# A diffusion layer on one core: what VectorE and ScalarE do ahead of what at its beginning, and where the step decays of its scan are computed

## The chip, the cores and the metric

The kernel runs on one core of a Trainium2 chip. It is one launch. The metric is the device time of that launch in microseconds (us), the median of three runs; smaller is better. A core has five engines that run side by side, each on its own queue of instructions in order: TensorE (PE, matrix products), VectorE (DVE), ScalarE (ACT), GpSimd (POOL) and SyncE (SP, which here issues the transfers). They wait for each other by semaphores.

## The reference

One layer of a diffusion model, for 512 latent tokens and 128 context tokens of width 1024. Both are normed and modulated by a conditioning vector, run through three mixers side by side (attention, a gated short convolution, a bidirectional state-space scan called SSD), each gated, summed and projected; a SwiGLU feed-forward part follows.

```python
def trunk_layer(x, mod, latent, ...):
    shift1, scale1, gate1, shift2, scale2, gate2 = jnp.split(mod, 6, axis=-1)   # mod = silu(c) @ ada_w + ada_b
    h = rms_norm(x, norm1_g) * (1.0 + scale1) + shift1
    mixed, k, v, s = token_mixers(h, latent, ...)
    x = x + gate1 * mixed
    ...
def token_mixers(h, latent, ...):
    proj = h @ w_in
    (q, k, v, conv_bg, conv_cg, conv_x, z, xbc, dt_raw, gate_logits) = jnp.split(proj, ...)
    ...
    dt = jax.nn.softplus(dt_raw + ssd_dt_bias)          # step sizes, 64 per token (2 directions x 32 heads)
    a = -jnp.exp(ssd_a_log)
    y_f, s_f = ssd_chunked(xs, dt[:, :, 0], a[0], bm, cm, s0[:, 0])
    ...
def ssd_chunked(x, dt, a, bm, cm, s0):
    acs = jnp.cumsum(dt * a, axis=2)                    # per chunk of 128 tokens
    decay = jnp.exp(where(causal, acs_i - acs_j))
    to_end = jnp.exp(acs[:, :, -1:] - acs)
    chunk_decay = jnp.exp(acs[:, :, -1])
    ...
```

## The kernel before

**Data.** The 640 tokens stay in SBUF, transposed: width in 8 blocks of 128 partitions (`KB`), tokens along the free axis. For precision each factor of a product is held as two parts, a high part cast to fp32r and a low part that is what the cast left out; a product is then three matmuls (high·high, high·low, low·high). `split` makes the parts: a cast on ScalarE (L166) and a subtraction on VectorE (L167). Every weight that comes in as a raw tile (`wr`, `ws`) is split so into `wh` and `wl` before TensorE can use it.

**Order.** Most of the program is placed by a tile scheduler. In the beginning, `manual_schedule` makes TensorE, VectorE and ScalarE take their instructions in the order in which the code is written. SP issues loads in program order, and waits where a buffer isn't free.

**Beginning** (pool `start`, L397 to L494). The x blocks, the conditioning columns and one 1 MB modulation matrix for each block (`modulation_load`, tile `aw`) are loaded. The squares of x are summed, `rstd` makes the norm's factor per token, and `rowcast` spreads it over the partitions as the row `rr` (TensorE L349, then VectorE's copy L351). A loop over the 8 blocks in the order `ORDER` then has, in pass n:
- `products(n)`: 16 small matmuls of the modulation matrix (L438) and ScalarE's copy of their result, `ms` (L440);
- in pass 0 `rowcast`'s row;
- `parts_of(n-1)`: the high part of the normed block before (ScalarE L458) and its low part (VectorE L459);
- `scaled(n)`: x times rr on VectorE (L455);
- the matmuls of the first gate (`EARLY`) on block n-2 (`streamed`, L311);
- `factors(n)`: four small matmuls on ms (L446), two small VectorE rows for shift and scale (`mod` L447, `A` L449), and the normed block `hf`: 512 columns on ScalarE (L451), 128 on VectorE (L452).

The first gate's weights, two raw tiles of 512 KB, are loaded behind the second modulation matrix and split in pass 1, after block 0's parts. Those of a second gate (`PLAIN[0]`) are split in pass 5, and seven of its eight blocks (`fill`) are done in the last two passes.

**Step decays.** `decays` is a generator: every `yield` hands back to the code that draws it with `next`. It projects the step sizes on TensorE (L513), transposes them, takes the softplus by a series on VectorE with an exponential on ScalarE, sums them along each chunk by products with triangles of ones, and leaves `cd`, `nlc`, `dte` in SBUF and the rows D_a and D_e in DRAM, for the SSD stage alone. Its four scratch tiles come from the shared slots (`slot`, 128 x 640). In before all of it is drawn inside the gated conv, between conv's units.

**Conv and attention.** The conv's units multiply and convolve on VectorE (`uv`, `g`, L162, L589) and sum some weights' parts on GpSimd (L229). Attention follows in the pool `att`: K projection, V projection in five token blocks (its parts `vh`, `vl`; the last block also copied as `vo` and stored), then the four Q projections of two heads each. `heads_norm_rope` copies a token block, takes its norm (`rms`, `rr` on GpSimd) and rotates it (`raw`, `rot`); `q_T` and `keys_T` transpose on TensorE (L745) and split. `rot`, `vo` and the squares `sq` share three buffers (tag `tmp`).

Of the kernel before, what the change touches and what calls it, by code (L numbers as in the profile page):

```python
# [15 lines left out]
P = 128  # L16
D = 1024
KB = D // P
# [67 lines left out]
def layer_kernel(  # L86
# [6 lines left out]
    nc = tc.nc  # L93
# [302 lines left out]
    with tc.tile_pool(name="start", bufs=10, reuse_waits="tile") as sp:  # L396
# [14 lines left out]
        modulation_load(ORDER[0])  # L411
        nc.sync.dma_start(par, cols)
        modulation_load(ORDER[1])
        raws = [qraw(w_gt[EARLY], a) for a in range(2)]
# [42 lines left out]
        def parts_of(k):  # L457
            act.copy(h[k].hi, hf[k])  # L458
            dve.tensor_tensor(h[k].lo, hf[k], f32(h[k].hi), op=sub)  # L459
# [6 lines left out]
        fill = None  # L466
        for n in range(KB + 2):
            if n + 3 < KB:
                modulation_load(ORDER[n + 3])
            if n < KB:  # L470
                products(ORDER[n])
            if n == 0:
                rr = rowcast(rs, TOKBLKS, sp)
            if 1 <= n <= KB:
                parts_of(ORDER[n - 1])
            if n == 1:
                we = Quarters([qsplit(raw) for raw in raws])
                raws = [qraw(w_gt[PLAIN[0]], a) for a in range(2)]
            if n == 5:
                wf, fill = Quarters([qsplit(raw) for raw in raws]), acc()  # L480
                raws = [qraw(w_gt[PLAIN[1]], a) for a in range(2)]
            if n < KB:
                scaled(ORDER[n])
            if n >= 2:
                for m in range(2):
                    streamed(early[m], we, m, n - 2)
            if n < KB:
                factors(ORDER[n])
            if n == KB - 1:
                streamed(fill, wf, 0, *range(4))  # L490
            if n == KB:
                streamed(fill, wf, 0, *range(4, 7))
        nc.sync.dma_start(wdt, w_dt)
        nc.sync.dma_start(rws, rows.unsqueeze(0).to_broadcast([P, rows.shape[0]]))  # L494
# [8 lines left out]
    dve.tensor_scalar(cw2[:, 96:], pv_["xcb"], 0.5, None, op0=mult)  # L503

    def decays():
# [16 lines left out]
        t4 = [slot() for _ in range(4)]  # L522
# [24 lines left out]
        yield  # L547
        pa = mx()
# [7 lines left out]
        dve.tensor_copy(tot, pt[:, :N])  # L556
        yield
# [39 lines left out]
    with tc.tile_pool(name="pj", bufs=2, reuse_waits="tile") as pj:  # L597
# [71 lines left out]
        for i in range(4):  # L669
            for j, _ in enumerate(conv_units(i)):  # L670
                next(dec, None)
            if i % 2:
                gate_unit(*todo.pop(0))
                next(dec, None)
        run(dec)
# [11 lines left out]
    with tc.tile_pool(name="att", bufs=2, reuse_waits="tile") as ap:  # L687
        cs = ap.tile([P, 8 * P], F32, name="cs", bufs=1)
        nc.sync.dma_start(cs, consts[:, C_COS:])
# [849 lines left out]
```

## Time and profile before

| what | value |
|---|---|
| runs | 1725.39, 1725.76, 1726.85 us; median 1725.76 |
| profiled execution | 1725.58 us, of which the span of its instructions is 1723.8 |
| TensorE busy | 1688.1 us (98% of the span), 11826 matmuls |
| VectorE busy | 1295.2 us (75%), 2330 instructions |
| ScalarE busy | 762.5 us (44%), 1437 instructions |
| GpSimd busy | 289.9 us (17%), 257 instructions |

Busy means that an instruction of the engine was running; a TensorE that is busy may still run at its lower clock, which the columns named PEclk or clk tell (1.00 is 2.4 GHz, 0.50 is 1.2 GHz). "x" is a count of instructions. A row of the timeline ends in brackets with the idle time of the engine ahead of it, and the instruction that ended that time.

### The profile page before, as it was taken

The numbers are of one execution on the slowest core, as the hardware profiler recorded it, in microseconds if no ns is written. First come the engines' busy times: TensorE is split into PE (matmuls) and PEld (weight loads), VectorE is DVE, ScalarE is ACT, GpSimd is POOL, SyncE is SP. The second block draws the span as 40 slices with busy tenths as digits, with TensorE's granted clock in tenths as the row PEclk, the third lists the DMA queues.
The fourth block names the chain that finished last, engine by engine and source line by source line (L and its number), as shares of the span: only waits on it lengthen the run. The fifth ranks groups of instructions, "written<-read, shape, count | busy, mean of one in ns | idle before, by whom it ended". The sixth has DMA issues, their size and how long they took to land.

```text
span 1723.8 us, 30050 instructions
## 1 busy us (share of the span) xinstructions
PE 1688.1 (98%) x11826; PEld 1643.1 (95%) x11826; DVE 1295.2 (75%) x2330; ACT 762.5 (44%) x1437; POOL 289.9 (17%) x257
## 2 busy tenths in 40 slices
PE   6999999999999999999999999999999999999998
PEld 4889999999999999999999999999999999999998
DVE  5779785786546778878886589994578676757898
ACT  4534434565454655555555332312355332424442
POOL 0234441110001111111001000000001231323432
PEclk9999999999999999999999999999999999999999
DMA  8322334211243534454444589763441222222222
GB/s 329 116 77 89 124 102 135 80 41 61 75 141 104 162 117 143 144 158 136 139 153 135 180 302 307 260 219 98 154 147 47 95 74 86 74 86 95 67 74 97
DMA packets 126974, 225.05 MB, mean 131 GB/s; under 512 B 9200, under 2 KB 69488, under 8 KB 125808
## 3 DMA queue, kind: packets, MB, share of 16 engines
q1 hardware_dynamic: 126832, 223.12, 39.6%
q8 instruction: 93, 1.52, 0.4%
q14 instruction: 49, 0.40, 0.1%
HBM read 199.43 MB, written 23.66 MB: 129 GB/s over the span
## 4 chain that ended last, share of the span: by engine, by line
PE 84%; DVE 10%; issue 3%; ACT 1%; DMA 1%; POOL 1%; SPq 0%; DVEq 0%; POOLq 0%; ACTq 0%
PE acc L311 41%; PE mx L250 21%; PE mx L311 7%; DVE wl L167 2%; PE acc L1277 2%; PE mx L1012 2%; PE mx L964 2%; PE mx L1018 1%; PE acc L778 1%; PE mx L298 1%; PE mx L299 1%; PE mx L297 1%; PE mx L990 1%; PE acc L794 1%; PE mx L941 1%
## 5 line engine op out<-in xcount | busy, mean ns | idle before, releaser
L311 PE MATMUL acc<-h,wh 128*128 128x320 f32 x2528 | 480.8, 312 | 0.2 <-ACT s L583 0.2
L311 PEld LDWEIGHTS acc<-h,wh 128*128 128x128 f32 x2528 | 394.8, 188 | 3.2 <-issue 2.7
L166 ACT CAST wh<-wr 128x1024 fp32r<-128x1024 f32 (+2 forms) x224 | 217.0, 971 | 322.6 <-PE acc L311 139.6
L167 DVE TENSOR_TENSOR wl<-wr,wh 128x1024 fp32r<-128x1024 f32 (+2 forms) x224 | 274.4, 1227 | 97.2 <-ACT wh L166 95.8
L311 PE MATMUL acc<-h,wl 128*128 128x320 f32 x1264 | 289.1, 310 | 0.0
L311 PEld LDWEIGHTS acc<-h,wl 128*128 128x128 f32 x1264 | 211.9, 188 | 0.0
L250 PE MATMUL mx<-h,wh 128*128 128x320 f32 x824 | 183.5, 310 | 0.0
L250 PE MATMUL mx<-s,wh 128*128 128x320 f32 x720 | 159.7, 309 | 1.5 <-DVE g L162 1.3
L311 PE MATMUL acc<-s,wh 128*128 128x320 f32 x768 | 152.7, 309 | 0.0
L986 ACT ACTIVATE ex<-rw,nlc 128x128 f32<-128x128 f32 x320 | 102.7, 394 | 106.2 <-DVE M L988 53.1
L166 ACT CAST wh<-ws 128x512 fp32r<-128x512 f32 (+3 forms) x111 | 82.6, 747 | 127.4 <-PE mx L250 64.1
L250 PEld LDWEIGHTS mx<-h,wh 128*128 128x128 f32 x824 | 138.0, 188 | 0.7 <-issue 0.5
L980 POOL TENSOR_SCALAR_AFFINE_SELECT rw<-rw 128x512 f32<-128x512 f32 x80 | 57.5, 742 | 465.0 <-DMA rw<-D_a 442.9
L250 PE MATMUL mx<-h,wl 128*128 128x320 f32 x412 | 127.3, 309 | 0.0
L311 PEld LDWEIGHTS acc<-s,wh 128*128 128x128 f32 x768 | 123.0, 188 | 0.3 <-ACT s L169 0.3
L250 PEld LDWEIGHTS mx<-s,wh 128*128 128x128 f32 x720 | 120.3, 188 | 2.3 <-DVE g L162 1.5
L250 PE MATMUL mx<-s,wl 128*128 128x320 f32 x360 | 111.2, 309 | 0.0
L167 DVE TENSOR_TENSOR wl<-ws,wh 128x512 fp32r<-128x512 f32 (+3 forms) x111 | 100.2, 904 | 8.3 <-ACT wh L166 7.3
L250 PE MATMUL mx<-T,wh 128*128 128x320 f32 x448 | 100.4, 312 | 4.4 <-DVE uv L162 4.4
L311 PE MATMUL acc<-s,wl 128*128 128x320 f32 x384 | 97.9, 309 | 0.0
L311 PE MATMUL mx<-s,wh 128*128 128x320 f32 x512 | 95.9, 309 | 0.0
L1136 DVE CUSTOM_DVE_ANT_0 jk<-aw,cr 128x512 f32<-128x512 f32 x128 | 88.1, 689 | 2.8 <-DMA aw<-in_ada_dram 0.4
(304 smaller groups left out, 3289.7 us busy)
## 6 DMA issues: line engine op xcount, KB each, us to landing
wr<-in_w_f_dram SPq DMA_DIRECT2D x60, 512.0 KB, 3.6
rw<-D_a SPq DMA_DIRECT2D x40, 512.0 KB, 3.8
aw<-in_ada_dram SPq DMA_DIRECT2D x64, 256.0 KB, 4.1
wr<-in_w_gt_dram SPq DMA_DIRECT2D x24, 512.0 KB, 3.7
wr<-in_w_cv_dram SPq DMA_DIRECT2D x24, 512.0 KB, 3.6
aw<-in_ada_dram SPq DMA_DIRECT2D x8, 1024.0 KB, 11.3
wr<-in_w_x_dram SPq DMA_DIRECT2D x16, 512.0 KB, 3.6
wr<-in_w_bc_dram SPq DMA_DIRECT2D x16, 512.0 KB, 3.6
```

The source lines that it names most:

```text
L166: act.copy(hi_t, src)
L167: dve.tensor_tensor(lo_t, src, f32(hi_t), op=sub)
L250: pe.matmul(out, y, z, start=not more and i == 0 and j == 0, stop=i == n - 1 and j == 2, skip_group_check=True)
L297: pe.matmul(out, l.hi, r.hi, start=start, stop=False)
L298: pe.matmul(out, l.hi, r.lo, start=False, stop=False)
L311: pe.matmul(bank(ps, e), x, y[:, e * HT:(e + 1) * HT], start=first and i == start and j == 0, stop=last and i == k - 1 and j == 2)
L964: pe.matmul(ps[:, d0 * GW:d1 * GW], xb[:, c, GW:], xw.pop(c)[:, d0:d1, :], start=True, stop=True)
L980: pool.affine_select(rw[:, d], rw[:, d], pattern=[[0, HPG], [1 - 2 * d, P]], compare_op=ALU.is_ge, fill=-1e4, base=0, channel_multiplier=2 ...
L986: act.activation(ex[:, d, r, :], rw[:, d, r, :], AF.Exp, bias=nlc[:, c, j:j + 1])
L1012: pe.matmul(pf[:, q * P:(q + 1) * P], pv[:, c, d, m * P:(m + 1) * P], b["C"][:, tok], start=True, stop=True)
L1136: dve.tensor_tensor_reduce(jk, aw, cr[:, s, :], 0.5, 0.0, op0=mult, op1=add, accum_out=mp[:, q, m, s:s + 1])
L1277: pe.matmul(ps[:, e, :HT], y, z, start=i == 0 and j == 0, stop=i == KB - 1 and j == 2)
```

## The change

Two parts. In the beginning, the order in a pass is another: the high part of the block before stands ahead of the products' copy, and `scaled` ahead of the low part. The first gate's weights are loaded ahead of the second modulation matrix and are split in pass 0, ahead of the copy of rr. The second gate's weights are loaded in pass 3 (with the small tiles `wdt` and `rws`, ahead of the last modulation matrix); one of their casts is done in the last pass, the rest of their split after the loop, and their matmuls between and behind those of the first gate's last two blocks. In the second part, only the first piece of `decays` (the projection) stays at the start of the conv; the rest is drawn in attention, one piece after each of V's token blocks and each block of the first two Q projections, with its scratch in a tag of attention's pool.

```diff
@@ beginning
         modulation_load(ORDER[0])
+        raws = [qraw(w_gt[EARLY], a) for a in range(2)]
         nc.sync.dma_start(par, cols)
         modulation_load(ORDER[1])
-        raws = [qraw(w_gt[EARLY], a) for a in range(2)]
         modulation_load(ORDER[2])
...
-        def parts_of(k):
+        def high(k):
             act.copy(h[k].hi, hf[k])
+
+        def low(k):
             dve.tensor_tensor(h[k].lo, hf[k], f32(h[k].hi), op=sub)
...
-        for n in range(KB + 2):
+        for n in range(KB):
             if n + 3 < KB:
                 modulation_load(ORDER[n + 3])
-            if n < KB:
-                products(ORDER[n])
+            if n == 3:
+                raws = [qraw(w_gt[PLAIN[0]], a) for a in range(2)]
+                nc.sync.dma_start(wdt, w_dt)
+                nc.sync.dma_start(rws, rows.unsqueeze(0).to_broadcast([P, rows.shape[0]]))
+            if n:
+                high(ORDER[n - 1])
+            products(ORDER[n])
             if n == 0:
+                we = Quarters([qsplit(raw) for raw in raws])
                 rr = rowcast(rs, TOKBLKS, sp)
-            if 1 <= n <= KB:
-                parts_of(ORDER[n - 1])
-            if n == 1:
-                we = Quarters([qsplit(raw) for raw in raws])
-                raws = [qraw(w_gt[PLAIN[0]], a) for a in range(2)]
-            if n == 5:
-                wf, fill = Quarters([qsplit(raw) for raw in raws]), acc()
-                raws = [qraw(w_gt[PLAIN[1]], a) for a in range(2)]
-            if n < KB:
-                scaled(ORDER[n])
+            if n == KB - 1:
+                wf, fill = [wtiles((2, 4, P)) for _ in range(2)], acc()
+                act.copy(wf[0].hi, raws[0])
+            scaled(ORDER[n])
+            if n:
+                low(ORDER[n - 1])
             if n >= 2:
                 for m in range(2):
                     streamed(early[m], we, m, n - 2)
-            if n < KB:
-                factors(ORDER[n])
-            if n == KB - 1:
-                streamed(fill, wf, 0, *range(4))
-            if n == KB:
-                streamed(fill, wf, 0, *range(4, 7))
-        nc.sync.dma_start(wdt, w_dt)
-        nc.sync.dma_start(rws, rows.unsqueeze(0).to_broadcast([P, rows.shape[0]]))
+            factors(ORDER[n])
+        high(ORDER[KB - 1])
+        dve.tensor_tensor(wf[0].lo, raws[0], f32(wf[0].hi), op=sub)
+        low(ORDER[KB - 1])
+        split(wf[1].hi, wf[1].lo, raws[1])
+        wf = Quarters(wf)
+        raws = [qraw(w_gt[PLAIN[1]], a) for a in range(2)]
+        for m in range(2):
+            streamed(early[m], we, m, KB - 2)
+        streamed(fill, wf, 0, 0, 2, 4)
+        for m in range(2):
+            streamed(early[m], we, m, KB - 1)
+        streamed(fill, wf, 0, 6, 1, 3, 5)
@@ decays: scratch, and two more yields
-        t4 = [slot() for _ in range(4)]
+        t4 = [slot(dec_pool[0], "dec", bufs=4) for _ in range(4)]
@@ conv
         dec = decays()
         next(dec)
         for i in range(4):
-            for j, _ in enumerate(conv_units(i)):
-                next(dec, None)
+            run(conv_units(i))
             if i % 2:
                 gate_unit(*todo.pop(0))
-                next(dec, None)
-        run(dec)
@@ attention, V projection
             split(vv.hi[:, t, :], vv.lo[:, t, :], pq[:, :256])
+            next(dec, None)
@@ attention, first two Q projections (and run(dec) behind the second)
         for n, _ in enumerate(queries(0)):
+            next(dec, None)
             if n in (1, 3):
                 keys_T(n // 2)
```

**ScalarE in the beginning**, from the first copy `ms` on (`hf` is the normed block, `h` its high part, `wh` the high parts of the first gate's weights). Before:

```order
L440 COPY ms_207<-mx_198 128x256
L451 ACTIVATE hf_104<-s_121,mod_74,A_76 128x512
L440 COPY ms_236<-mx_227 128x256
L458 CAST h_85<-hf_104 128x640
L166 CAST wh_240<-wr_143 128x1024
L166 CAST wh_244<-wr_145 128x1024
L451 ACTIVATE hf_108<-s_125,mod_74,A_76 128x512
L440 COPY ms_271<-mx_262 128x256
L458 CAST h_93<-hf_108 128x640
```

and after the change:

```order
L440 COPY ms_207<-mx_198 128x256
L166 CAST wh_209<-wr_140 128x1024
L166 CAST wh_213<-wr_142 128x1024
L451 ACTIVATE hf_104<-s_121,mod_74,A_76 128x512
L458 CAST h_85<-hf_104 128x640
L440 COPY ms_245<-mx_236 128x256
L451 ACTIVATE hf_108<-s_125,mod_74,A_76 128x512
L458 CAST h_93<-hf_108 128x640
L440 COPY ms_268<-mx_259 128x256
```

The two casts of the gate's weights (L166) have moved from behind the first block's high part to the place behind the first ms, and each high part (L458) now stands ahead of the next ms (L440).

**VectorE in the beginning**, from the norm's `rms` on (`s_215` and `s_223` are the row rr, `wl` the low parts of the first gate's weights). Before:

```order
L341 TENSOR_SCALAR rms_189<-acc_182 128x5
L351 COPY s_215<-acc_209 128x640
L455 TENSOR_TENSOR s_121<-s_121,s_215 128x640
L447 TENSOR_TENSOR mod_74<-mx_218,par 128x4
L449 TENSOR_SCALAR A_76<-mod_74,par 128x2
L452 TENSOR_SCALAR hf_104<-s_121,A_76,mod_74 128x128
L459 TENSOR_TENSOR h_86<-hf_104,h_85 128x640
L167 TENSOR_TENSOR wl_241<-wr_143,wh_240 128x1024
L167 TENSOR_TENSOR wl_245<-wr_145,wh_244 128x1024
L455 TENSOR_TENSOR s_125<-s_125,s_215 128x640
```

and after the change (L461 is the low part, L459 in before):

```order
L341 TENSOR_SCALAR rms_189<-acc_182 128x5
L167 TENSOR_TENSOR wl_210<-wr_140,wh_209 128x1024
L167 TENSOR_TENSOR wl_214<-wr_142,wh_213 128x1024
L351 COPY s_223<-acc_217 128x640
L455 TENSOR_TENSOR s_121<-s_121,s_223 128x640
L447 TENSOR_TENSOR mod_74<-mx_226,par 128x4
L449 TENSOR_SCALAR A_76<-mod_74,par 128x2
L452 TENSOR_SCALAR hf_104<-s_121,A_76,mod_74 128x128
L455 TENSOR_TENSOR s_125<-s_125,s_223 128x640
L461 TENSOR_TENSOR h_86<-hf_104,h_85 128x640
```

The two low parts of the gate's weights stand ahead of the copy of rr (L351), and the scaling of the second block (L455 on s_125) ahead of the first block's low part.

**VectorE in attention's V projection** (`vl` are the low parts of V's token blocks, `wl` those of the weights of the second Q projection). Before:

```order
L726 TENSOR_TENSOR raw_2748<-raw_2748,rot_2934 128x256
L167 TENSOR_TENSOR vl<-mx_2954,vh 128x256
L167 TENSOR_TENSOR vl<-mx_2981,vh 128x256
L167 TENSOR_TENSOR vl<-mx_3008,vh 128x256
L167 TENSOR_TENSOR vl<-mx_3035,vh 128x256
L167 TENSOR_TENSOR wl_3332<-wr_3329,wh_3331 128x1024
L167 TENSOR_TENSOR wl_3338<-wr_3335,wh_3337 128x1024
L167 TENSOR_TENSOR vl<-mx_3062,vh 128x256
L760 COPY vo<-mx_3062 128x256
```

and after the change, from the second token block's low part on (`dec` are the scratch tiles of the step decays):

```order
L544 TENSOR_TENSOR dec_2921<-dec_2921,dec_2923 128x320
L167 TENSOR_TENSOR vl<-mx_2958,vh 128x256
L545 TENSOR_TENSOR dec_2922<-dec_2921 128x320
L547 TENSOR_SCALAR dec_2923<-dec_2922 128x320
L549 SCALAR_TENSOR_TENSOR dec_2923<-dec_2923,dec_2922 128x320 x4
L167 TENSOR_TENSOR vl<-mx_2990,vh 128x256
L549 SCALAR_TENSOR_TENSOR dec_2923<-dec_2923,dec_2922 128x320 x3
L552 SCALAR_TENSOR_TENSOR dec_2923<-dec_2923,dec_2921 128x320
L167 TENSOR_TENSOR wl_3316<-wr_3313,wh_3315 128x1024
L167 TENSOR_TENSOR wl_3322<-wr_3319,wh_3321 128x1024
L167 TENSOR_TENSOR vl<-mx_3019,vh 128x256
L772 COPY vo<-mx_3019 128x256
```

The series of the softplus (L544 to L552) stands between the low parts of V, ahead of the last of them and of the copy `vo`.

## Rows read from the trace of the kernel before

**Rows 1.** The page's chain of work that ended last, by engine

```profile
PE 84%; DVE 10%; issue 3%; ACT 1%; DMA 1%; POOL 1%; SPq 0%; DVEq 0%; POOLq 0%; ACTq 0%
```

**Rows 2.** Windows: stretch, length, busy of PE/PEld/DVE/ACT/POOL (instructions), clock, DMA share, GB/s

```profile
20.20:61.40 41.20, 36.54 (x279) 29.87 (x280) 29.35 (x60) 19.77 (x34) 1.37 (x1) 0.88 0.56 217
23.10:29.90 6.80, 6.72 (x35) 5.26 (x35) 4.57 (x7) 4.25 (x7) 0.00 (x0) 0.50 1.01 391
47.00:50.40 3.40, 3.40 (x23) 2.13 (x23) 2.21 (x5) 1.44 (x4) 0.00 (x0) 0.50 0.62 229
100.00:180.00 80.00, 75.63 (x502) 74.51 (x501) 76.31 (x102) 31.62 (x45) 34.49 (x23) 0.98 0.28 96
125.50:128.90 3.40, 3.40 (x14) 3.40 (x14) 3.40 (x7) 0.44 (x1) 0.29 (x1) 0.50 0.42 154
292.90:303.40 10.50, 10.50 (x90) 10.50 (x89) 4.71 (x9) 3.23 (x6) 0.00 (x0) 1.00 0.22 68
303.40:322.30 18.90, 18.52 (x156) 18.28 (x154) 12.67 (x39) 10.42 (x40) 3.92 (x5) 1.00 0.28 96
```

**Rows 3.** Timeline of TensorE: start, us, work, [idle before <-releaser]

```profile
23.18 1.01 PE L446 MATMUL mx<-comb,ms 128*128 128x2 f32 x4 [1.88 <-ACT ms L440]
...
46.45 0.61 PE L446 MATMUL mx<-comb,ms 128*128 128x2 f32 x4 [2.59 <-ACT ms L440]
...
125.27 0.72 PE L250 MATMUL mx<-T,wh 128*128 128x320 f32 x2 [2.76 <-DVE uv L162]
...
178.23 0.56 PE L250 MATMUL mx<-T,wh 128*128 128x320 f32 x2 [0.53 <-DVE uv L162]
...
322.45 0.41 PE L745 MATMUL acc<-cst,raw 128*128 128x128 f32 x2 [0.53 <-ACT sq L734]
```

**Rows 4.** Chain of waits, 30 to 40: start, us, what

```profile
34.42 0.73 DVE s L455
...
38.08 0.73 DVE s L455
```

**Rows 5.** Timeline of TensorE, products of two passes

```profile
30.14 1.07 PE L438 MATMUL mx<-aw,cz 128*32 128x256 f32 x16
...
33.52 1.07 PE L438 MATMUL mx<-aw,cz 128*32 128x256 f32 x16
```

**Rows 6.** Timeline of ScalarE and VectorE at the beginning

```profile
17.73 0.37 ACT L440 COPY ms<-mx 128x256 f32<-128x256 f32 x1 [5.36 <-PE mx L438]
...
20.00 0.82 DVE L351 COPY s<-acc 128x640 f32<-128x640 f32 x1 [4.00 <-PE acc L349]
...
22.06 0.81 ACT L451 ACTIVATE hf<-s,mod,A 128x512 f32<-128x512 f32 x1 [3.96 <-DVE A L449]
...
23.66 1.99 ACT L166 CAST wh<-wr 128x1024 fp32r<-128x1024 f32 x2
...
24.73 2.36 DVE L167 TENSOR_TENSOR wl<-wr,wh 128x1024 fp32r<-128x1024 f32 x2
```

**Rows 7.** DMA issues from 9.4 to 9.8: KB each, us to landing

```profile
wr<-in_w_gt_dram SPq DMA_DIRECT2D x1, 512.0 KB, 10.5
```

**Rows 8.** Windows of VectorE, tiles s alone: busy, clock, DMA share, GB/s

```profile
100.00:145.00 45.00, 19.17 (x19) 0.96 0.24 86
```

**Rows 9.** One source line: ns least/median/most, first and last start

```profile
L538 DVE SCALAR_TENSOR_TENSOR s<-s,s x7: 476/1471/1584, 115.8 to 140.3; 128x320 f32<-128x320 f32 x7
```

**Rows 10.** Timeline of VectorE, the reciprocal

```profile
106.37 2.15 DVE L531 RECIPROCAL s<-s 128x320 f32<-128x320 f32 x1
```

**Rows 11.** Lines of TensorE, 100 to 210: busy us, mean ns

```profile
L552 PE MATMUL mx<-s,cst 128*128 128x32 f32 x20 | 2.3, 272 | 0.0
```

**Rows 12.** Timeline of VectorE, first rotation of the queries

```profile
308.44 0.49 DVE L723 TENSOR_TENSOR rot<-raw,cs 128x128 f32<-128x128 f32 x2 [2.42 <-DMA out_dram<-vo]
```

**Rows 13.** Timeline of ScalarE, a change of its tables

```profile
177.13 1.28 ACT L620 ACT_TABLE_LOAD   x1
...
178.43 0.44 ACT L620 ACTIVATE g<-mx 128x320 f32<-128x320 f32 x1
```

More of the change, by code (lines that the diff above doesn't have):

```diff
@@ L465, in layer_kernel @@
         early = [(mx(), mx()) for _ in range(2)]
-        fill = None
-        for n in range(KB + 2):
+        for n in range(KB):
             if n + 3 < KB:
                 modulation_load(ORDER[n + 3])
-            if n < KB:
-                products(ORDER[n])
+            if n == 3:
[5 more added lines that the diff above has]
+            products(ORDER[n])
             if n == 0:
+                we = Quarters([qsplit(raw) for raw in raws])
                 rr = rowcast(rs, TOKBLKS, sp)
-            if 1 <= n <= KB:
-                parts_of(ORDER[n - 1])
-            if n == 1:
-                we = Quarters([qsplit(raw) for raw in raws])
-                raws = [qraw(w_gt[PLAIN[0]], a) for a in range(2)]
-            if n == 5:
-                wf, fill = Quarters([qsplit(raw) for raw in raws]), acc()
-                raws = [qraw(w_gt[PLAIN[1]], a) for a in range(2)]
-            if n < KB:
-                scaled(ORDER[n])
+            if n == KB - 1:
[4 more added lines that the diff above has]
+                low(ORDER[n - 1])
             if n >= 2:
@@ L503, in layer_kernel @@
     dve.tensor_scalar(cw2[:, 96:], pv_["xcb"], 0.5, None, op0=mult)
+    dec_pool = []
     def decays():
@@ L547, in decays @@
         yield
+        yield
         pa = mx()
@@ L556, in decays @@
         dve.tensor_copy(tot, pt[:, :N])
+        yield
         yield
@@ L689, in layer_kernel @@
         nc.sync.dma_start(cs, consts[:, C_COS:])
+        dec_pool.append(ap)
         cos = lambda t: cs[:, t * P:(t + 1) * P]
@@ L858, in layer_kernel @@
         for n, _ in enumerate(queries(1)):
+            next(dec, None)
             if n in (1, 3):
                 qTs[n // 2] = q_T(raws[0][0], n // 2)
+        run(dec)
         banks.close()
```

## Prediction

> **What bounds the kernel now.** I read the chain of waits first: followed back from the last instruction, 84% of the span is TensorE and 10% VectorE [rows 1]. So a saving counts only where it shortens a time in which TensorE is idle or runs at its low clock; work taken off VectorE or ScalarE is worth nothing by itself. The table by stages then says where such time lies among the places that the change touches [rows 2]. In the beginning, 20.20 to 61.40, TensorE is busy for 36.54 of 41.20 us, so 4.66 idle, and two stretches stand at 0.50, which is the 1.2 GHz level (6.72 and 3.40 us of work). In the gated conv, 100 to 180, it is busy for 75.63 of 80.00, so 4.37 idle, with VectorE at 76.31 of 80, and a stretch of 3.40 stands at 0.50. In attention's V projection and the first Q projection (292.9 to 322.3) TensorE idles for only 0.38, while VectorE has 5.79 and 6.23 us free.
>
> An idle wait can cost twice. The waits of 1.88 us before 23.18, of 2.59 before 46.45 and of 2.76 before 125.27 [rows 3] each stand at the head of one of the three low stretches. A microsecond of work at the low level costs half a microsecond against the high one: 3.4, 1.7 and 1.7 us.
>
> **Beginning: the order inside a pass.** Each pass over one of the 8 blocks does 16 products, a copy of their result, a scaling, the factors, the norm's output and its parts. The chain of waits there repeats every 3.66 us: from the scaling L455 at 34.42 to that at 38.08 [rows 4]. It runs low part, scaling (0.73), mod, A, hf, copy ms (0.37, as at 17.73 [rows 6]), high part, low part. The change puts scaling ahead of the low part, and the high part ahead of the copy, so these two pieces leave the loop: 3.66 - 0.73 - 0.37 = 2.56. TensorE's own pass, from products at 30.14 to products at 33.52, is 3.38 [rows 5]. The chain falls below that; then TensorE sets the pace and waits no more within a pass. What scaling and copy cost is the same as before; they hide under TensorE's 3.38, and without that cover the two would cost 1.10 a pass.
>
> **Beginning: the first gate's weights.** In before they are split after the first block's parts: casts of 1.99 us at 23.66, low parts of 2.36 from 24.73. Now both stand ahead of the copy of the norm's row rr, which in before starts at 20.00 [rows 6]. When can they start? The second half of these weights lands 10.5 us after an issue at about 9.7 [rows 7], so at 20.2; now it is ahead of a 1 MB modulation column, and at the 391 GB/s of that time [rows 2] a megabyte takes 2.7 us: landing at about 17.4 (an estimate). ScalarE's copy ms ahead of the casts ends at about 18.1, so the casts take 18.1 to 20.1 and the last low part ends at about 21.3. The copy of rr then starts 1.3 us later than 20.00, and VectorE's rr, scaling, mod and A (0.82, 0.82, 0.15, 0.23 and their gaps) bring hf to 23.4 where it was 22.06. Behind hf (0.81) now stands the high part (about as long) and only then the copy ms on which TensorE's next factors wait: 25.3 where it was 23.18. So the first idle time grows from 1.88 to about 4.0. The modulation column put behind the weights lands at about 20.2, just when its products start at 20.24; if it is late by up to 4 us, that lies in the same idle time.
>
> **Beginning: the second gate's weights.** Their split stood in pass 5 on both engines; behind it the copy ms came so late that TensorE waited 2.59 us [rows 3]. Now one cast stands in the last pass and the rest behind the loop, where TensorE has the sixth and seventh blocks of the first gate to do. The idle time goes, and with it the low stretch from 47.0. Their load now stands ahead of the last modulation column in SP's queue, together with the small weights of the step projection; at the rate above the 1 MB of weights puts that column back by 2.7 us, which is less than one pass.
>
> Sum: TensorE's work between 20.2 and 61.4 at the high level is 36.54 - 3.4 - 1.7 = 31.4. With 4.0 idle and one low stretch as long as the first of before (3.4 lost), the work ends at 20.2 + 31.4 + 4.0 + 3.4 = 59.0: **-2.4 us**. Bounds: nothing gained if a third wait comes (the fill's weights late by 2 us); -4.5 if the wait stays at 1.9.
>
> **Conv: the chain of step decays leaves.** Between conv's products, VectorE does 19 instructions of this chain between 100 and 145, 19.17 us in all [rows 8], and a few more later. The same form takes 476 ns at the least and 1584 at the most [rows 9]; the reciprocal takes 2.15 [rows 10]. Without 19.17 of 45 us VectorE is free for conv's own products, on whose low parts and multiplications TensorE waits (2.76 <- uv L162 at 125.27). TensorE's 4.37 idle and 1.7 of low clock go, but the wait at 178.23 has no decay row ahead of it: it ends a chain from GpSimd's sum through a cast. I leave 0.5 for it: -4.4 - 1.7 + 0.5 = **-5.6 us**; bounds -6.1, and -2.4 if only the wait of 2.76 shrinks to 0.4 and the clock stays. Some of TensorE's work (20 small products of the cumulative sums, 2.3 [rows 11], and as I estimate by their number another 1.3 of the same kind) moves from here to attention, which changes nothing in the sum.
>
> **Attention: the chain arrives.** It stands in VectorE's queue between the low parts of V's five token blocks: 16 of its instructions now stand ahead of the copy vo. 15 at 476 ns, 2.15 for the reciprocal and one round through ScalarE's exponential (0.5) are 9.8 us; VectorE's free time there is 5.8 [rows 2], so vo is late by 4.0. The store of vo frees a buffer for the rotation of the first queries: rot at 308.44 waits 2.42 us for it [rows 12], and would start 4.0 later against TensorE's own work. Behind it, up to 322.3, five more instructions come in (2.9 us, four at 476 ns and a strided one that I take as 1.0), the low parts of the keys and of the cached values (1.1) have moved ahead into the wait, and I take 1.5 of the 6.2 free microseconds as filled: the last q block is ready 4.0 + 2.9 - 1.1 - 1.5 = 4.3 us later. TensorE's transposes there wait 0.53 already (322.45 [rows 3]); its own new work ahead of them, the 3.6 just named, gives cover. So a wait that grows by about 0.7: **+0.6 us**. Bounds: -0.5 (even the present wait goes) and +4 (nothing is filled, and low clock of 1.7 follows). ScalarE has the time: 3.23 + 10.42 busy of 29.4 there.
>
> The exponentials and the logarithm need ScalarE's tables changed as often as before, now between attention's casts. The row shows 1.28 us for a load, and the next activation 0.02 behind its end [rows 13]. I count 1.28 each, hidden in ScalarE's free time. The Trainium skill (ScalarE: Activation LUTs, What ACT_TABLE_LOAD costs) gives a switch about 2.66 us, a load and a drain of like size; the row shows no such drain. By that rule two switches would hold ScalarE 2.8 us longer, and if TensorE saw all of it the sum would be -4.6 instead of -7.4; I give it a twentieth, inside the case of a late attention.
>
> **Sum.** -2.4 - 5.6 + 0.6 = -7.4, on the profiled execution's 1725.58 (the median of the runs is 1725.76, 0.2 above, and the same to this accuracy): **1718.2 us**.
>
> **The rivals.** (a) The beginning gives nothing: the longer first idle time brings a low stretch longer by as much as the second one saved, or the second gate's weights come late. For it: the idle time doubles. Against it: both waits lie far apart, and only one is kept. 1725.6 - 5.6 + 0.6 = 1720.6. (b) The conv's waits stay in part, because GpSimd's sums and the casts behind them set them, as at 178.23: only 2.4 of the large wait and the clock's 1.7 go, giving 1725.6 - 2.4 - 4.1 + 0.6 = 1719.7; were the clock to stay low too, and with (a), 1725.6 - 2.4 + 0.6 = 1723.8, no change. Against it: the long waits stand in the time of the chain. (c) Slower: attention cannot take the chain. Were its instructions there as dear as in conv (about 1.0 us each, 19.17 for 19, and not half that), VectorE would be late by another 11 us over its 21 instructions, no longer covered; with a low stretch of 1.7 it is 1718.2 + 12.7 = 1731. For it: vo's store stands behind the chain and the rotation behind the store. Against it: GpSimd is busy for 3.92 of those 29.4 us, in conv for 34.49 of 80 [rows 2]. It decides from some 10.9 us of lateness beyond the forecast's (7.4 and the 3.45 that a measurement needs); at 7.4 the kernel is unchanged. (d) Better: the first idle time stays short or the low stretch does, and attention is at its good bound: 1725.6 - 4.5 - 6.1 - 0.5 = 1714.5.
>
> **How the numbers follow.** Forecast 0.52, (a) 0.12, (b) 0.10, both 0.05, attention late by 3 to 10 us 0.08, (c) 0.04, (d) 0.09. The forecast's own terms spread it over 1716 to 1720.5. The range reaches to (d) with a margin and past the two half cases: 1713 to 1722.5. A measurement here tells changes from about 0.2%, 3.45 us. Faster by more than that: forecast, (a), (b), (d), about 0.83; within it: both, and most of late attention, 0.12; slower 0.05.
>
> **What would show it.** Passes of the beginning at TensorE's pace, about 3.4 us, with one wait near 25 us and no low stretch near 47; the gate's casts at 18 and low parts ended by 21.5. Idle time of TensorE in the conv below 1 us, and no stretch at 0.50 there. In attention vo's copy near 307 less what the earlier stages saved, rot about 4 us later relative to TensorE's projections, and a wait below 1.5 us at the q transposes. Wrong would be: weights that land after 19 us, a low stretch at attention's beginning, or conv waits that end on a cast behind a GpSimd sum.

## The result, and the profile after

The changed kernel takes 1711.91 us (median of four runs, 1711.54 to 1713.08) where the kernel before took 1725.58 (1722.52 to 1726.85): a ratio of 0.9925, interval 0.9913 to 0.9937, so 10.9 to 15.0 us less. The forecast was 1718.2 with a range from 1713.0: right in its sign, little more than half of what was measured, and outside its range by 1.1 us. The profiled executions, 1725.58 before and 1713.08 after, lie 12.5 apart, and it is these 12.5 us that the traces can account for.

Where they came from is read from where TensorE begins a stage. The projection of the step sizes follows the beginning, attention's K projection follows the conv, and the products C·B begin the SSD stage. The rows of these three lines of TensorE, first before (L513, L297, L990), then after (L524, L297, L1005); behind the colon stand the least, median and most ns of one, then the first and the last start in us:

```profile
L513 PE MATMUL mx<-hf,wdt x32: 432/432/483, 83.6 to 87.7; 128*64 128x320 f32 x32
...
L297 PE MATMUL mx<-wh,h x240: 280/283/387, 271.4 to 403.5; 128*128 128x256 f32 x120
...
L990 PE MATMUL mx<-C,B x80: 270/275/377, 540.4 to 968.3; 128*128 128x128 f32 x80
```

```profile
L524 PE MATMUL mx<-hf,wdt x32: 432/432/483, 79.8 to 83.9; 128*64 128x320 f32 x32
...
L297 PE MATMUL mx<-wh,h x240: 278/283/521, 257.0 to 392.2; 128*128 128x256 f32 x120
...
L1005 PE MATMUL mx<-C,B x80: 270/275/377, 527.4 to 955.7; 128*128 128x128 f32 x80
```

The beginning ends 3.8 us earlier (83.6 to 79.8). From there to the K projection it is 187.8 before and 177.2 after: 10.6 less. From K to SSD 269.0 and 270.4: 1.4 more. Work of TensorE has moved from the conv to attention in between; the lines of TensorE of after, 274 to 309, with busy us and mean ns:

```profile
L564 PE MATMUL mx<-dec,cst 128*128 128x32 f32 x20 | 2.3, 272 | 0.0
...
L567 PE MATMUL mx<-dec,cst 128*128 128x320 f32 x2 | 0.8, 474 | 0.0
L582 PE MATMUL acc<-cst,dec 128*64 128x128 f32 x5 | 0.7, 272 | 0.0
L532 PE MATMUL mx<-cst,s 64*128 64x64 f32 x5 | 0.5, 233 | 0.0
```

That is 4.3 us. So the conv itself gave 10.6 - 4.3 = 6.3, and the stretch from attention to the SSD stage 4.3 - 1.4 = 2.9; the rest of the kernel lost 0.5. The windows of after that answer to [rows 2] (the first is the beginning, from the second products up to the place that was 61.40 in before):

```profile
20.50:57.60 37.10, 33.20 (x280) 28.24 (x280) 27.92 (x60) 19.32 (x34) 0.69 (x1) 0.91 0.64 250
23.60:30.40 6.80, 4.83 (x27) 3.54 (x28) 4.24 (x9) 3.62 (x6) 0.00 (x0) 0.50 1.01 418
100.00:180.00 80.00, 80.00 (x547) 80.00 (x546) 66.75 (x90) 33.17 (x47) 39.63 (x25) 1.00 0.33 112
...
279.20:293.10 13.90, 13.90 (x119) 13.90 (x117) 12.99 (x26) 6.11 (x13) 0.00 (x0) 1.00 0.18 49
293.10:311.00 17.90, 17.90 (x152) 17.74 (x151) 15.45 (x47) 12.51 (x38) 3.86 (x5) 1.00 0.32 101
```

TensorE is busy for all of 80 us in the conv, at the full clock, where it idled 4.37. In attention's V projection VectorE is nearly full (12.99 of 13.90) and TensorE never waits. In the beginning 3.90 us of idle time are left, all in one wait, and one stretch at 0.50. The timeline of after there:

```profile
18.27 1.99 ACT L166 CAST wh<-wr 128x1024 fp32r<-128x1024 f32 x2
19.35 2.36 DVE L167 TENSOR_TENSOR wl<-wr,wh 128x1024 fp32r<-128x1024 f32 x2 [3.08 <-ACT wh L166]
...
21.63 0.82 DVE L351 COPY s<-acc 128x640 f32<-128x640 f32 x1
...
23.68 0.81 ACT L451 ACTIVATE hf<-s,mod,A 128x512 f32<-128x512 f32 x1 [3.41 <-DVE A L449]
...
25.57 1.01 PE L446 MATMUL mx<-comb,ms 128*128 128x2 f32 x4 [3.90 <-ACT ms L440]
26.52 1.93 PE L438 MATMUL mx<-aw,cz 128*32 128x256 f32 x16
```

Read against [rows 6] and the first row of [rows 3], this is the chain that the prediction put together: low parts ended by 21.7, rr behind them, hf at 23.7 and TensorE's factors at 25.57 (forecast 21.3, 23.4, 25.3). The last row is at the low clock: the same 16 products take 1.07 at the high one [rows 5].

### The profile page after: what moved, and what is told of

It is laid out like the page before. It is cut to its first block, busy times and chain, and to the rows that moved or that the text cites. A ratio compares the mean times of both kernels' runs of the same rounds, so it can differ in the third digit from the quotient of the medians.

```text
span 1711.3 us, 30048 instructions
## 1 busy us (share of the span) xinstructions
PE 1680.5 (98%) x11826; PEld 1638.4 (96%) x11826; DVE 1289.0 (75%) x2330; ACT 762.1 (45%) x1437; POOL 293.1 (17%) x257
## 4 chain that ended last, share of the span: by engine, by line
PE 86%; DVE 8%; issue 2%; ACT 1%; DMA 1%; POOL 1%; SPq 0%; DVEq 0%; POOLq 0%; ACTq 0%
PE acc L311 42%; PE mx L250 23%; PE mx L311 8%; DVE wl L167 2%; PE acc L1292 2%; PE mx L1027 2%; PE mx L979 2%; PE mx L1033 1%; PE acc L790 1%; PE mx L1005 1%; PE acc L806 1%; POOL rr L342 1%; PE mx L298 1%; PE mx L956 1%; PE mx L299 1%
## 5 line engine op out<-in xcount | busy, mean ns | idle before, releaser
L166 ACT CAST wh<-wr 128x1024 fp32r<-128x1024 f32 (+1 forms) x223 | 216.1, 971 | 327.0 <-PE acc L311 159.0
L167 DVE TENSOR_TENSOR wl<-wr,wh 128x1024 fp32r<-128x1024 f32 (+1 forms) x223 | 273.0, 1226 | 97.4 <-ACT wh L166 96.0
L166 ACT CAST wh<-ws 128x512 fp32r<-128x512 f32 (+3 forms) x111 | 82.8, 747 | 130.6 <-PE mx L250 66.9
L167 DVE TENSOR_TENSOR wl<-ws,wh 128x512 fp32r<-128x512 f32 (+3 forms) x111 | 101.6, 917 | 10.6 <-ACT wh L166 9.6
```

The costliest lines, as they stand in the source:

```text
L166: act.copy(hi_t, src)
L167: dve.tensor_tensor(lo_t, src, f32(hi_t), op=sub)
```

## The experiments

Twelve runs beside the first two: ten kernels, one of them twice (e4b), and the changed kernel again (a2). Each was timed against the kernel before on its own chip. Their chips differ, so they are compared by the ratio to before. The last two columns come from each profiled execution: the start of the step projection (L513 in before), and the time from the K projection's start to the first product C·B.

| kernel | median us | ratio to before, interval | step projection starts | K projection to C·B |
|---|---|---|---|---|
| before | 1725.58 | 1 | 83.6 | 269.0 |
| changed | 1711.91 | 0.9925 [0.9913, 0.9937] | 79.8 | 270.4 |
| e1, beginning alone | 1720.14 | 0.9976 [0.9967, 0.9985] | 79.1 | 267.2 |
| e2, decays alone | 1715.98 | 0.9950 [0.9937, 0.9962] | 83.3 | 270.2 |
| e3, series twice | 1719.84 | 0.9970 [0.9958, 0.9982] | 80.2 | 278.5 |
| e4, wait filled | 1712.15 | 0.9924 [0.9911, 0.9936] | 77.3 | 270.0 |
| e5, old order in a pass | 1714.21 | 0.9938 [0.9926, 0.9950] | 80.5 | 271.7 |
| e6, first split later | 1711.15 | 0.9927 [0.9915, 0.9939] | 79.1 | 270.0 |
| e7, second split in pass 5 | 1717.42 | 0.9959 [0.9946, 0.9972] | 87.1 | 270.3 |
| e8, products ahead | 1708.67 | 0.9910 [0.9898, 0.9923] | 77.2 | 269.8 |
| a2, changed again | 1713.41 | 0.9930 [0.9918, 0.9942] | 79.8 | 270.2 |
| e4b, wait filled again | 1711.38 | 0.9924 [0.9912, 0.9936] | 78.2 | 271.1 |
| e9, gate loads behind | 1709.15 | 0.9909 [0.9896, 0.9922] | 76.2 | 270.6 |
| e10, no series | 1713.14 | 0.9931 [0.9919, 0.9943] | 78.9 | 270.3 |

Five of these rows have one and the same beginning (changed, a2, e1, e3, e10), and their step projections start between 78.9 and 80.2. A difference of less than 1.3 us in that column tells nothing by itself.

**Each part alone.** e1 takes the change's first three pieces (loads, order in the loop, splits), e2 the others:

```diff
 e2, in the conv and in attention, on the kernel before
-            for j, _ in enumerate(conv_units(i)):
-                next(dec, None)
+            run(conv_units(i))
...
             split(vv.hi[:, t, :], vv.lo[:, t, :], pq[:, :256])
+            next(dec, None)
```

> The change's beginning alone; the decays stay in the conv as before. Theory (the two parts add up, and the beginning is worth what the traces of before and after show at the start of the conv, 83.6 against 79.8): 3.8 us faster than before, 1722 by a profiled run of 1725.6; TensorE waits once, about 3.9 us before 25.6, then one low stretch; the conv keeps idle time of about 4.4 us and its low stretch. Rival (the conv's waits move with the start, so the gain is lost there): within 1 us of before.

> The decays' move alone; the beginning is that of before. Theory (conv: idle 4.4 and low clock 1.7 go; attention: the wait of 0.53 at the q transposes goes): 6 us in the conv and 0.5 in attention, 1719 against 1725.6; if the low stretch behind the wait at 426 to 429 goes too, 1717.4. Rival (my prediction's step, attention's wait grows by 0.7): 1720.0, with a wait of over 1 us at the q transposes.

Measured, in the order of the two expectations: 0.24% and 0.50% less, together 0.74%, where the whole change has 0.75%. The two parts add up. In e1 the conv has its waits as in before (the view of who waits for whom, TensorE, 90 to 260: us in total, times, longest):

```profile
PE mx L250 <- DVE uv L162: 4.2, 3, 2.8
```

and in e2 the conv has none, while the two waits of the beginning stay. The same view of e2, from 15 to 290, has this one row:

```profile
PE mx L446 <- ACT ms L440: 4.5, 2, 2.6
```

No wait at the q transposes shows in e2. It is 8.6 us below before on its chip (1715.98 against 1724.56), near the 8.2 that the expectation gives where the stretch behind 426 to 429 goes too (1725.6 to 1717.4). The conv's part of the theory holds; the rival, a wait that grows in attention, falls.

**How much attention can take.** e3 computes the series of the softplus twice, 8 VectorE instructions more; e10 leaves it out:

```diff
 e3
+        for again in (True, False):
...
-            if j % 2 == 0:
-                yield
+                if j % 2 == 0 and not again:
+                    yield
 e10
-        dve.tensor_tensor(s2, u, u, op=mult)
...
-        for j in range(n - 1, 0, -1):
-            dve.scalar_tensor_tensor(q, q, 2.0 / (2 * j + 1), s2, op0=add, op1=mult)
...
+        dve.tensor_scalar(q, u, 2.0, None, op0=mult)
```

> The changed kernel with the softplus's series computed twice, 8 more VectorE instructions of about 0.49 us (3.9) in V's projection, ahead of the copy vo. Theory (VectorE's work there is late by 3.1 us against 3.6 of cover, so 0.5 is left): the q transposes come 3.9 later less what fills the free time of 1 to 2 us, a wait of 1.5 to 3.5 us appears there, and 1.7 of low clock if it is long: 2 to 5 us slower than the changed kernel. Rival (the queue has slack, the wait for the store of vo and for GpSimd takes it up): under 0.5 us slower, no wait there.

> The changed kernel with the softplus's series left out (one product by 2 stands for it): 9 VectorE instructions of about 0.49 us less in V's projection, TensorE's work as it is. Theory (attention hides the chain: no wait of TensorE hangs on it there): within 0.7 us of the changed kernel. Rival (vo, rotation and q transposes are on the path, as my prediction had it, with 4.3 us of lateness against 3.6): 0.7 to 2 us faster.

Without the series the kernel is as fast as with it (0.9931 against 0.9930 on the same chip): attention hides it. The ratios alone would not exclude the rival's smallest gain of 0.7, but the stretch from the K projection to C·B takes 270.3 us without the series and 270.2 with it (a2). With it twice, 3.9 us of work cost 0.45%, 7.7 us, twice the work and more than the theory's 2 to 5. The timeline of TensorE in e3, and the window behind its wait:

```profile
299.70 1.49 PE L565 MATMUL mx<-dec,cst 128*128 128x32 f32 x6 [3.72 <-DVE dec L558]
```

```profile
299.70:308.50 8.80, 8.79 (x38) 8.40 (x39) 5.19 (x19) 0.72 (x3) 1.74 (x2) 0.50 0.01 2
```

The wait is not at the q transposes. It is ahead of them, at the cumulative sums, which TensorE has in its own queue and which need the chain's product with the decay rate. That deadline was missing in my prediction. The 8.79 us of work behind the wait then run at the low clock and lose 4.4. How near the deadline is in the changed kernel, two rows of after tell:

```profile
293.50 0.49 DVE L557 TENSOR_TENSOR dec<-dec,av 128x320 f32<-128x320 f32 x1
...
295.61 2.31 PE L564 MATMUL mx<-dec,cst 128*128 128x32 f32 x20
```

The product with the decay rate ends at 293.99 and TensorE takes the first sum at 295.61, so 1.6 us are to spare.

**What the store of vo waits for.** e10 shows it beside the changed kernel, since SP issues in another order there. SP's timeline and the landing of vo's store (KB, us from issue to landing), first of after:

```profile
291.29 0.33 SPq L185 DMA_DIRECT2D wr<-in_w_q_dram  x1
291.67 0.42 SPq L775 DMA_DIRECT2D cv<-in_cacheV_dram  x1
293.10 0.34 SPq L773 DMA_DIRECT2D out_dram<-vo  x1
```

```profile
out_dram<-vo SPq DMA_DIRECT2D x1, 128.0 KB, 2.7
```

and the same two views of e10:

```profile
287.80 1.47 SPq L185 DMA_DIRECT2D wr<-in_w_q_dram  x2
289.60 0.34 SPq L768 DMA_DIRECT2D out_dram<-vo  x1
```

```profile
out_dram<-vo SPq DMA_DIRECT2D x1, 128.0 KB, 5.1
```

The same 128 KB take 5.1 us directly behind two 512 KB loads, and 2.7 where one such load and the 128 KB of cv were issued ahead of it (the second load is issued behind it). These are two executions and not a run that changes the order alone. In e10 the rotation waits 3.46 us for that store, and no wait of TensorE follows from it.

**The beginning's pieces.** Each of e5, e6 and e7 undoes one piece of it in the changed kernel:

```diff
 e5, order in a pass
+            products(ORDER[n])
             if n:
                 high(ORDER[n - 1])
-            products(ORDER[n])
...
-            scaled(ORDER[n])
             if n:
                 low(ORDER[n - 1])
+            scaled(ORDER[n])
 e6, first gate
-                we = Quarters([qsplit(raw) for raw in raws])
                 rr = rowcast(rs, TOKBLKS, sp)
...
                 low(ORDER[n - 1])
+            if n == 1:
+                we = Quarters([qsplit(raw) for raw in raws])
 e7, second gate
-            if n == KB - 1:
-                wf, fill = [wtiles((2, 4, P)) for _ in range(2)], acc()
-                act.copy(wf[0].hi, raws[0])
+            if n == 5:
+                wf, fill = [qsplit(raw) for raw in raws], acc()
```

> The changed kernel with the order inside a pass as before: the products' copy ahead of the high part, the low part ahead of scaling; both gates' splits as changed. Theory (the chain of 3.66 us against TensorE's 3.38 sets the pace): 0.28 us in each of six passes, 1.7 us slower than the changed kernel, as short waits on ms. Rival (the chain lost almost nothing in before either, 0.33 us of idle time between 30 and 43): under 0.5 us; and since the first ms copy comes ahead of the high part, TensorE's first wait is 0.7 shorter, so up to 0.7 faster.

> The changed kernel with the first gate's weights split in pass 1, behind the first block's low part, as before. Theory (the split ahead of rr is what makes the wait grow from 1.9 to 3.9): the wait ends near 23.9 instead of 25.6, and 0.5 us are lost where the low parts come late: about 1 us faster than the changed kernel. Rival (my prediction's sum, the split there holds up the second block's mod and A by 2.4 us and a second wait comes): 0 to 1.5 us slower.

> The changed kernel with both halves of the second gate's weights split in pass 5, as before. Theory (casts of 2 us ahead of a copy ms and low parts of 2.4 ahead of scaling bring back the wait before 46 and its low stretch): a wait of 2 to 2.6 us and 1.7 of low clock, 3.7 to 4.3 slower than the changed kernel. Rival (the shorter chain in a pass takes the split up): under 1 us slower, no low stretch near 47.

For e5 and e6 the last products of the loop divide the beginning better than its end does. They stand here, in the changed kernel and in e5:

```profile
44.75 1.07 PE L438 MATMUL mx<-aw,cz 128*32 128x256 f32 x16
```

```profile
43.75 1.07 PE L438 MATMUL mx<-aw,cz 128*32 128x256 f32 x16
```

From there to the step projection it is 35.1 us in the changed kernel (and 35.0 to 35.1 in the four others with its beginning), and 36.8 in e5. So the old order costs 1.7 us, the size that the theory gave, but not as a short wait in each pass: TensorE keeps its 3.3 us a pass up to these products, while VectorE's scaling repeats every 3.67 (33.56, 37.23, 40.90), and the whole loss lies behind them, 0.57 of it in two waits near 48 and 51. That TensorE lived until then on the lead that the first wait left is argued and not shown. The first wait of e5 is 3.18 instead of 3.90, the 0.7 of the rival. In the timed runs e5's ratio is 0.0013 above that of the changed kernel, inside the intervals. e6 brings the first wait down to 2.50 and ends it at 24.08, as the theory said, but its step projection (79.1) lies among the five and its ratio (0.9927) at that of the changed kernel: no run tells whether anything is gained. The rival's second wait did not come. e7 is the piece that matters: 0.9959, 0.34% or 5.9 us slower than the changed kernel. Its timeline and the window behind its wait:

```profile
45.79 0.90 PE L311 MATMUL mx<-h,wh 128*128 128x320 f32 x2 [2.43 <-DVE h L461]
```

```profile
45.80:55.10 9.30, 9.30 (x45) 8.01 (x46) 4.47 (x11) 3.62 (x6) 0.00 (x0) 0.50 0.22 70
```

2.43 us of wait and 4.65 of low clock: a wait and a low stretch come back as the theory said, though the wait ends on the low part of a normed block and not on a copy ms, and the stretch is nearly three times as long as in before, so the price is larger than its 3.7 to 4.3. Its runs lie in two groups, 1714 to 1715 and 1719 to 1720. A stretch of different length would give that; the profiled execution (1720.38) is of the slower group, and none of the faster was profiled.

**Does the wait bring the low clock?** e4 (and e4b, the same kernel) lets TensorE do 9 matmuls in the first wait, into a bank that the gate overwrites later:

```diff
+            if n == 1:
+                for _ in range(9):
+                    pe.matmul(early[0][0][:, :256], ident, cst[:, :256], start=True, stop=True)
             factors(ORDER[n])
```

> The changed kernel with 9 matmuls of 256 columns, whose result nothing reads, in TensorE's wait of 3.9 us before the second block's factors. Theory (the wait brings the low stretch): the stretch at 1.2 GHz behind it is gone, 2.3 us faster than the changed kernel, about 1709.6. Rival (the stretch comes from the start of the work and not from the wait): the stretch stays, the time stays within 0.5 us, or gets longer if the 9 matmuls last longer than the wait.

> The 9 matmuls in the wait once more, since five runs spread over 4.7 us. Theory (the wait brings the low stretch, and without the one the other goes): no low stretch in the beginning in the profile, and a median 1 to 2.3 us below the changed kernel of the same chip. Rival (the matmuls, 4.1 us for a wait of 3.9, and low stretches elsewhere eat it up): within 0.7 us.

> The changed kernel again, beside the next three on one chip. Both theories: 1711.5 to 1713 with one low stretch in the beginning; if the low stretch that the kernel before had behind the wait at 426 to 429 is a matter of the single run, one shows now and then behind the like wait at 416, 1.7 us longer.

TensorE's timeline of e4, behind these matmuls:

```profile
21.24 4.15 PE L493 MATMUL mx<-cst 128*128 128x256 f32 x18
...
25.81 1.07 PE L438 MATMUL mx<-aw,cz 128*32 128x256 f32 x16
```

The products behind the filled wait take 1.07 instead of 1.93, so it was the wait that brought the low clock, and the step projection starts 1.6 (e4b) to 2.5 us (e4) earlier than in the changed kernel, ahead of all five with its beginning. The timed runs do not resolve that: 0.9924 twice, against 0.9925 and 0.9930, inside the intervals; on the one chip that had both, e4b's median is 2.0 us below a2's. a2 came out at 1713.41, a little above what was expected of it, and its profiled execution has no low stretch near 416.

**A better order.** e8 puts each block's products one pass earlier, so that they stand ahead of the factors of the block before, and the first gate's low parts behind the second block's factors. e9 is e8 with the second gate's loads in pass 4 instead of 3, behind the last modulation matrix.

```diff
             if n:
                 high(ORDER[n - 1])
-            products(ORDER[n])
+            if n == 0:
+                products(ORDER[0])
+            elif n + 1 < KB:
+                products(ORDER[n + 1])
...
             factors(ORDER[n])
+            if n == 0:
+                products(ORDER[1])
+            if n == 1:
+                for w, raw in zip(we, early_raws):
+                    dve.tensor_tensor(w.lo, raw, f32(w.hi), op=sub)
+                we = Quarters(we)
```

> The changed kernel with each block's products one pass earlier, ahead of the factors of the block before, and the first gate's low parts behind the second block's factors instead of ahead of rr. Theory (the first wait hangs on low parts, rr and the copy ms in one chain): the next products fill 1.1 us of the wait, which ends near 24.0; 1.5 us faster than the changed kernel, 3 to 4 if the low stretch behind it goes too: 1708 to 1710.5. Rival (the third modulation matrix lands at 22.9, so the products wait for it and the matmuls of the gate for the low parts): within 0.7 us of the changed kernel.

> The kernel with products a pass earlier, and the loads of the second gate's weights and the two small tiles behind the last modulation matrix instead of ahead of it. Theory (TensorE's wait of 1.18 us at 39.27 is for that matrix): this wait goes, 1 us faster than 1708.7. Rival (the second gate's weights then land late and their split waits): within 0.5 us, or slower.

e8 is the fastest kernel here with e9: 0.9910, 1708.67 us, some 2.6 us below the changed kernel by the ratios, and the step projection starts at 77.2. The intervals still overlap, but all nine runs of e8 and e9 (up to 1710.22) lie below all ten of the changed kernel (from 1711.28); of these, e9 and a2 ran on one chip. TensorE's timeline of e8 shows that its first waits are now for loads, and that the products behind them take 1.07, at the high clock:

```profile
22.35 1.07 PE L438 MATMUL mx<-aw,cz 128*32 128x256 f32 x16 [0.62 <-DMA aw<-in_ada_dram]
23.36 0.61 PE L446 MATMUL mx<-comb,ms 128*128 128x2 f32 x4
24.85 1.07 PE L438 MATMUL mx<-aw,cz 128*32 128x256 f32 x16 [0.88 <-DMA aw<-in_ada_dram]
```

e9 removes the wait at 39.27 as expected (projection at 76.2), and the timed runs do not tell it from e8 (0.9909).

## Why the prediction was wrong in size

**Conv, -5.6: right, measured -6.3.** The 4.37 us of idle time and the low stretch went, as forecast. What failed was the 0.5 that I left for the wait at 178.23: it is gone too, also in e2, though no decay row stood directly ahead of it. In before the GpSimd sum of that chain itself waited 2.42 us for VectorE's low parts (at 173.43), so a freer VectorE can start it earlier; this is argued, and no run separates it.

**Beginning, -2.4: measured -3.8.** One wait of 3.90 and one low stretch came as computed, and the waits near 46 went. The failing piece is "one low stretch as long as the first of before (3.4 lost)". The stretch is as long, 6.8 us, but it begins at 23.6, two microseconds into the wait, and costs only on what runs in it: 4.83 us of work, 2.4 lost. With 0.76 less idle time and 5.1 - 2.4 = 2.7 less lost to the clock, 3.4 of the 3.8 are told; the other 0.4 are within what the same beginning varies by from one execution to the next (1.3). The pieces weigh otherwise than in the sum, too: the order inside a pass, which has no term of its own there, is worth 1.7 us behind the last products (e5), and the second gate's split, 2.6 of wait and 1.7 of clock in the sum, is worth 5.9 (e7).

**Attention, +0.6: measured -2.9.** This is the step that failed: rot that "would start 4.0 later" behind the store of vo, and from it "a wait that grows by about 0.7". VectorE's lateness was right at first: vo starts 10.3 us earlier than in before where the K projection starts 14.4 earlier, so 4.1 late (forecast 4.0). Rows of VectorE, before and after:

```profile
302.96 0.42 DVE L760 COPY vo<-mx 128x256 f32<-128x256 f32 x1
```

```profile
292.65 0.41 DVE L772 COPY vo<-mx 128x256 f32<-128x256 f32 x1
...
297.00 0.49 DVE L734 TENSOR_TENSOR rot<-raw,cs 128x128 f32<-128x128 f32 x2
```

But rot at 297.00 is 11.4 earlier than in before [rows 12], so late by 3.0 and not 4.0, since it no longer waits for the store: I had let rot move with vo, as if the store took the same time (4.9 us in before), and it took 2.7 at its new moment. At the q transposes, the last rotation in before and after, and TensorE's transposes in after:

```profile
321.88 0.42 DVE L726 TENSOR_TENSOR raw<-raw,rot 128x256 f32<-128x256 f32 x1
```

```profile
310.62 0.42 DVE L737 TENSOR_TENSOR raw<-raw,rot 128x256 f32<-128x256 f32 x1
...
310.96 0.71 PE L756 MATMUL acc<-cst,raw 128*128 128x128 f32 x5
```

Against the K projection the rotation is 3.1 late, where the forecast had 4.3 for the last q block. TensorE has all 4.3 us of the moved work ahead of these transposes and not 3.6, and starts them 3.9 later than in before (from 321.43). So the wait of 0.53 there [rows 3] went instead of growing. That is 1.1 of the 3.5 that this step is off. The lateness is read from the rows; no run changes the store alone. Another 1.7 was never the change's: the profiled execution of before has a low stretch from 429.3, behind two waits of 1.02 together that the changed kernel has too, at 416, without the stretch. The windows of before there, and the stretch of e5, whose attention is that of the changed kernel:

```profile
426.00:429.30 3.30, 2.28 (x16) 1.70 (x15) 2.17 (x6) 3.18 (x6) 0.00 (x0) 1.00 0.01 2
429.30:432.70 3.40, 3.40 (x14) 3.36 (x15) 1.01 (x3) 0.46 (x2) 0.00 (x0) 0.50 0.92 291
```

```profile
418.50:421.90 3.40, 3.40 (x15) 3.36 (x15) 0.91 (x3) 0.38 (x2) 0.00 (x0) 0.50 0.90 281
```

The stretch behind these waits comes in two of the fourteen profiled executions, one with either version of attention. e1, with attention as in before, has the waits and not the stretch, and goes from the K projection to C·B in 267.2 us where before took 269.0. My sum was made against an execution that had it, so 1.7 us of its time were chance, and what the change itself gave in attention is nearer 1.2 than 2.9. The remaining 0.7 of the step are not assigned.

**ScalarE's tables.** The forecast priced a load at 1.28 and let it be hidden. In after the loads stand at 290.64 and 298.52 and the activations behind them wait 2.41 and 1.28 us for VectorE, not for the table:

```profile
290.64 1.28 ACT L578 ACT_TABLE_LOAD   x1
294.33 0.47 ACT L578 ACTIVATE dec<-dec 128x320 f32<-128x320 f32 x1 [2.41 <-DVE dec L577]
...
301.08 0.47 ACT L572 ACTIVATE cd<-dec 128x320 f32<-128x320 f32 x1 [1.28 <-DVE dec L568]
```

So the load is off the path here. The Trainium skill (ScalarE: Activation LUTs, What ACT_TABLE_LOAD costs) counts a drain beside it; these rows neither show nor exclude one, since the engine waits anyway.

**The range.** The good case (d) was put at 1714.5 and given 0.09, with the low end at 1713.0. Conv and attention came out past their good bounds (-6.1 and -0.5) and the beginning well on its good side (-3.8, with -4.5 as the bound), all at once. 1.7 of attention's 2.9 were chance, and the changed kernel's median lies another 1.2 below its profiled execution (1711.91 against 1713.08). Had the execution that I started from been without that stretch, forecast and range would have lain 1.7 lower, and the measured time inside. The slower rival (c) did not come: in attention the chain's 24 instructions take 12.28 us of VectorE where 19 of them took 19.17 in the conv [rows 8]; in the conv GpSimd is busy for 34.49 of 80 us beside it [rows 2], and one form of instruction takes 476 to 1584 ns [rows 9]. Two rows of before, of GpSimd and of that form, and then the window of VectorE in after on the tiles of the decays alone:

```profile
118.54 2.08 POOL L229 TENSOR_TENSOR ws<-ws,wr 128x512 f32<-128x512 f32 x1 [3.26 <-DVE wl L167]
...
119.39 3.10 DVE L538 SCALAR_TENSOR_TENSOR s<-s,s 128x320 f32<-128x320 f32 x2
```

```profile
278.00:303.00 25.00, 12.28 (x24) 1.00 0.28 85
```

The four dear instructions of that form (about 1.5 us each, two from 119.39 and two from 134.93) ran while GpSimd added, and the three of 0.48 (at 115.79, 139.55 and 140.35) while it was idle. In after GpSimd has no work between 278.0 and 294.1, and all seven take about 0.5. No run takes the sums away alone, so the times agree with this cause and do not prove it.

## What to carry to other kernels

Move a long chain of small VectorE work to a stage in which TensorE is fed from far ahead and GpSimd is quiet; there it was hidden and an instruction took half the time, but with 1.6 us to spare, less than one more series (3.9), and its first deadline was the chain's own products in TensorE's queue. Price a transfer that a wait hangs on by what is queued around it at its new moment, not by what it took at the old one. And count a low stretch by the work that runs in it, and as chance where the same wait stands in another run without it. The best cure found here was to give TensorE the next block's work to do in the wait; e8 does that and moves the low parts too, so the share of each is not known.

## What the runs showed of the hardware

How long TensorE stays at the 1.2 GHz level behind a wait is not told by the wait alone. Behind 2.43 us (e7) 9.3 us of work ran at 0.50, behind 3.72 (e3) 8.8, behind 2.59 in before 3.4 and behind 1.88 there 6.7 [rows 2, 3], and behind 1.0 either 3.4 or none. The clock column can also be silent: in a2 it shows no stretch below 1.00 in the beginning, while the products behind a wait of 2.69 take 1.94 us, the time of the low level. The length of the rows themselves is the surer sign:

```profile
25.23 1.01 PE L446 MATMUL mx<-comb,ms 128*128 128x2 f32 x4 [2.69 <-ACT ms L440]
26.17 1.94 PE L438 MATMUL mx<-aw,cz 128*32 128x256 f32 x16
```
